# A hybrid RWKV-7 and sparse-attention layer: raised norms and masks, values behind transposes, and three reordered sums

## The chip, the core and the metric

The kernel runs on one core of one Trainium2 chip. The metric is the device time of one launch in microseconds (us), from the first to the last thing the core does. The engines have their own instruction queues: TensorE (PE) multiplies matrices into PSUM, VectorE (DVE) and ScalarE (ACT) work element by element and move PSUM results to SBUF, GpSimd (POOL) does a few small steps and issues some of the DMAs, SyncE (SP) issues most of the DMAs.

## The reference

One decoder layer on x of 1024 tokens by 1024 channels, float32. A projection feeds two mixers side by side; their outputs are gated, merged and followed by a feed-forward network (FFN).

```python
u = rmsnorm(x, norm1_g); p_rwkv, p_att, p_idx, p_gate = split(u @ w_in)
# RWKV-7, 8 heads of 64, on token-shifted p_rwkv: r, k, v, decay w, a, gate g
kk = (k * k_k) / max(norm(k * k_k, per head), 1e-12)
k = k * (1 + (a - 1) * k_a);  decay = exp(-exp(w))
# per token: sa = state @ -kk;  y = state @ r  after
state = state * decay + sa x (kk * a) + v x k
y_a = (groupnorm(y) + sum(r * k * r_k) * v) * g
# attention, 8 heads of 64: rope(q), rope(k), v; each query keeps the 256 keys
# with the highest indexer scores, softmax over them
y_b = dsa_attention(q, k, v, q_idx, k_idx, w_idx)
h = x + (sigmoid(g_a) * (y_a @ w_o_rwkv) + sigmoid(g_b) * (y_b @ w_o_att)) @ w_out
z_gate, z_up = split(rmsnorm(h, norm2_g) @ w_ffn_in)
h = h + (silu(z_gate) * z_up) @ w_ffn_out
return rmsnorm(h, normf_g)
```

## The kernel before

**Arithmetic.** Channels lie on the 128 partitions, tokens on the free axis, in two halves of 512 tokens. Each large matrix product is made of three products of values that are split into a high and a low part (`split`, L114 on ScalarE for the high part and L115 on VectorE for the low one): high × high (L140), high × low activation (L141), low weight × high (L145), in `mm3`. `mm3_last` (L149 to L158) puts the products that need the last block of the activations behind all others, for one or two outputs at a time. Weights come by DMA into `wst` and are split on the way.

**Order.** The order of TensorE's queue is that of the program (`manual_schedule`). The instructions of the other engines are put in order by a list scheduler when the kernel is built: among instructions that are ready by its own estimate it takes those within `tc.high_priority()` first, and otherwise the order of the program counts; on the chip each engine then runs its queue strictly in the order built. `weights` is in high priority already. `tc.issue_after(x)` keeps an instruction behind x in the built order.

**Filler.** RWKV is a chain of small dependent steps. `rwkv` runs it in four quarters of 256 tokens (q = 0 to 3; q = 0 and 1 are half 0), and between two steps it calls `pump(n)`, which takes work worth about n matmuls from the deque `fill`: projections in quarter 0, then projections of the gates (`proj_gates`), attention of half 0 blended with more gates (`blend`, 2 steps of one and 2 of the other), and from the middle of quarter 2 on (`ready`) the merge and the FFN of half 0. Attention of half 1 and the second merge and FFN come after RWKV. `ticks` pumps and also advances the late part of the indexer's selection (L944 among its lines) on VectorE and ScalarE.

**The steps of a quarter** that matter here: the sums of squares of the key per head (`sums`); the clamp into `nq` (L589, VectorE); two transposes of nq (L593, TensorE); the copy of 16 columns into `nr` (L595, VectorE); the power (L599, GpSimd); its split; two transposes (L604); the copy into `nrT` (L606, ScalarE); the spread back over channels (L612, TensorE) and the multiply into kk. Then come the operands AR (L630, L631) and BK (L637, L640) on VectorE, multiplies with the decays P and their inverse Pi. `km` is the key times its factor, multiplied ahead of the sums. Behind a pump follow eight masks in four pairs: TensorE makes products of BK and AR (L667) in two PSUM buffers, VectorE multiplies them with `cmask` into MT (L671); four groups of transposes of BK (L686) are copied into NAT by ScalarE (L689).

**PSUM.** `acc()` has three buffers, for large products; `mix()` has five, for everything else. A matmul into a buffer waits until its last reader is done.

**Attention** (`attend`) goes over 16 units of a half, (head pair, block of 128 queries). In one pass of the loop it makes the logits of unit i for two heads (L1029, reduced with the bias on VectorE in L1031, the exponential in L1034), transposes those of unit i-1 (`turn`, L1043, copied in L1045) and multiplies those of unit i-2 with v (`values`, L1053), with a `yield` behind each, at which the filler runs. The last results go through memory to `d_yb` (L1068 to L1090).

**The ends.** `merge` loads y (the RWKV half in blocks 0 to 3, the attention half in 4 to 7), splits it and multiplies it with `w_o`, the two halves into two accumulators (L1158 reads the first). `ffn_out` adds the FFN's output to h; the last of the three groups (`final`) also sums the squares of h (`Rms.add`) for the last norm. In half 1 this is `finish_out`, in two runs of 256 tokens. `Rms.columns` sums the squares over the partitions by a matmul with ones (L241) and takes the power on GpSimd.

## Time and profile before

| | |
|---|---|
| time, median of 3 runs | 1748.55 us (1747.58 to 1753.21) |
| the profiled execution's own time | 1748.71 us |
| its span | 1746.9 us |
| granted TensorE clock, mean | 0.996 |
| TensorE busy, matmuls | 1708.1 us, 98% |
| TensorE weight loads | 1410.3 us, 81% |
| VectorE busy | 1114.3 us, 64% |
| ScalarE busy | 833.3 us, 48% |
| GpSimd busy | 100.5 us, 6% |
| moved by DMA | 247.14 MB, 141 GB/s |

The page of the profile gives busy times and the chain of work that ended last. The list of waits has one row for each pair of a waiting instruction and what released it: the sum of the waits in us, how many, and the longest. The timeline has the start and the duration of each instruction, and in brackets how long its engine had been idle before it and what released it. The windows give the busy time of each engine in a stretch and the clock that TensorE was granted. The groups (by line and shape) give the total and the mean in ns.

### The profile page before, as it was taken

The numbers are of one execution on the slowest core, as the hardware profiler recorded it, in microseconds if no ns is written. First come the engines' busy times: TensorE is split into PE (matmuls) and PEld (weight loads), VectorE is DVE, ScalarE is ACT, GpSimd is POOL, SyncE is SP. The second block draws the span as 40 slices with busy tenths as digits, with TensorE's granted clock in tenths as the row PEclk, the third lists the DMA queues.
The fourth block names the chain that finished last, engine by engine and source line by source line (L and its number), as shares of the span: only waits on it lengthen the run. The fifth ranks groups of instructions, "written<-read, shape, count | busy, mean of one in ns | idle before, by whom it ended". The sixth has DMA issues, their size and how long they took to land.

```text
span 1746.9 us, 26692 instructions
## 1 busy us (share of the span) xinstructions
PE 1708.1 (98%) x10156; PEld 1410.3 (81%) x10156; DVE 1114.3 (64%) x2133; ACT 833.3 (48%) x1547; POOL 100.5 (6%) x123
## 2 busy tenths in 40 slices
PE   8999999999999998999999999999999999999997
PEld 6888888778878776878787888888788888888887
DVE  6789899857468567857876655445465564454464
ACT  6365998453445687645333455433234322232241
POOL 0000000010021111000100321000000000000000
PEclk9999999999999999999999999999999999999999
DMA  5542224536357535644343765173464344434442
GB/s 210 173 138 94 97 97 145 163 97 171 100 178 201 149 121 157 197 146 118 97 127 93 234 165 138 61 225 113 165 213 140 109 136 151 136 96 150 139 124 93
DMA packets 132383, 247.14 MB, mean 141 GB/s; under 512 B 36848, under 2 KB 60080, under 8 KB 132128
## 3 DMA queue, kind: packets, MB, share of 16 engines
q1 hardware_dynamic: 108896, 171.61, 31.7%
q10 hardware_dynamic: 15552, 47.75, 8.7%
q0 software_dynamic: 7808, 26.09, 5.6%
q8 instruction: 80, 1.31, 0.3%
q14 instruction: 47, 0.39, 0.1%
HBM read 192.40 MB, written 53.00 MB: 140 GB/s over the span
## 4 chain that ended last, share of the span: by engine, by line
PE 50%; issue 1%; DVE 1%; ACT 0%; POOLq 0%; POOL 0%; DVEq 0%; ACTq 0%
PE acc L145 14%; PE acc L140 13%; PE acc L141 13%; PE acc L156 3%; PE mix L1053 1%; PE mix L1029 1%; PE mix L1043 1%; PE acc L1197 0%; PE mix L800 0%; PE mix L788 0%; PE acc L1201 0%; ACT whi L114 0%; DVE h L1272 0%; PE mix L254 0%; PE mix L810 0%
## 5 line engine op out<-in xcount | busy, mean ns | idle before, releaser
L115 DVE TENSOR_TENSOR wlo<-wst,whi 128x1024 fp32r<-128x1024 f32 (+1 forms) x229 | 277.5, 1214 | 276.0 <-PE acc L145 132.7
L114 ACT ACTIVATE whi<-wst 128x1024 fp32r<-128x1024 f32 (+1 forms) x229 | 238.3, 1043 | 262.7 <-PE acc L141 186.9
L140 PE MATMUL acc<-zhi,whi 128*128 128x512 f32 x672 | 264.8, 394 | 0.0
L141 PE MATMUL acc<-zlo,whi 128*128 128x512 f32 x672 | 262.0, 390 | 0.0
L145 PE MATMUL acc<-zhi,wlo 128*128 128x512 f32 x672 | 170.2, 392 | 0.0
L140 PEld LDWEIGHTS acc<-zhi,whi 128*128 128x128 f32 x672 | 126.2, 188 | 26.8 <-issue 1.9
L141 PEld LDWEIGHTS acc<-zlo,whi 128*128 128x128 f32 x672 | 126.3, 188 | 24.8
L145 PEld LDWEIGHTS acc<-zhi,wlo 128*128 128x128 f32 x672 | 124.8, 188 | 25.4 <-issue 0.7
L140 PE MATMUL acc<-u1hi,whi 128*128 128x512 f32 x352 | 140.5, 399 | 0.1
L141 PE MATMUL acc<-u1lo,whi 128*128 128x512 f32 x352 | 137.6, 391 | 0.0
L140 PE MATMUL acc<-u0hi,whi 128*128 128x512 f32 (+1 forms) x352 | 135.5, 387 | 1.7 <-DVE tmp L323 1.7
L141 PE MATMUL acc<-u0lo,whi 128*128 128x512 f32 (+1 forms) x352 | 133.8, 383 | 0.0
L140 PE MATMUL acc<-fhi,whi 128*128 128x512 f32 (+1 forms) x318 | 114.3, 368 | 2.3 <-ACT whi L114 1.5
L141 PE MATMUL acc<-flo,whi 128*128 128x512 f32 (+1 forms) x318 | 112.9, 364 | 0.2 <-DVE flo L115 0.2
L145 PE MATMUL acc<-u1hi,wlo 128*128 128x512 f32 x352 | 90.0, 394 | 0.0
L145 PE MATMUL acc<-u0hi,wlo 128*128 128x512 f32 (+1 forms) x352 | 85.7, 384 | 0.0
L114 ACT ACTIVATE fhi<-tmp 128x512 fp32r<-128x512 f32 x44 | 27.7, 630 | 112.6 <-DVE tmp L1229 112.3
L140 PEld LDWEIGHTS acc<-u0hi,whi 128*128 128x128 f32 x352 | 66.2, 188 | 14.9 <-ACT stg L114 2.1
L140 PEld LDWEIGHTS acc<-u1hi,whi 128*128 128x128 f32 x352 | 66.2, 188 | 14.8 <-issue 1.3
L141 PEld LDWEIGHTS acc<-u1lo,whi 128*128 128x128 f32 x352 | 66.2, 188 | 12.6
L141 PEld LDWEIGHTS acc<-u0lo,whi 128*128 128x128 f32 x352 | 66.2, 188 | 12.1
L145 PEld LDWEIGHTS acc<-u1hi,wlo 128*128 128x128 f32 x352 | 64.9, 188 | 13.7 <-issue 0.9
(328 smaller groups left out, 3204.2 us busy)
## 6 DMA issues: line engine op xcount, KB each, us to landing
wst<-in_w_ffn_in SPq DMA_DIRECT2D x72, 512.0 KB, 3.6
wst<-in_w_in ACTq DMA_DIRECT2D x36, 512.0 KB, 4.5
wst<-in_w_in SPq DMA_DIRECT2D x27, 512.0 KB, 4.0
wst<-in_w_fo SPq DMA_DIRECT2D x25, 512.0 KB, 3.8
k<-d_k POOLq DMA_DIRECT2D x24, 512.0 KB, 7.9
h<-in_xT SPq DMA_DIRECT2D x32, 256.0 KB, 5.2
d_g<-tmp ACTq DMA_DIRECT2D x32, 256.0 KB, 3.4
tmp<-d_g SPq DMA_DIRECT2D x32, 256.0 KB, 3.7
```

Of the source, the lines that this page charges most:

```text
L114: A.activation(hi, x, AF.Copy)
L115: V.tensor_tensor(lo, x, hi.bitcast(F32), op=ALU.subtract)
L140: T.matmul(ps, whi[:, wk + k, :], ahi[:, ak + k, tok], start=k == 0, stop=False)
L141: T.matmul(ps, whi[:, wk + k, :], alo[:, ak + k, tok], start=False, stop=False)
L145: T.matmul(ps, wlo[:, wk + k, :], ahi[:, ak + k, tok], start=False, stop=k == nk - 1)
L156: T.matmul(ps, w[:, k, :], a[:, k, tok], start=k == 0 and w is whi and a is ahi, stop=k == nk - 1 and a is alo)
L1029: T.matmul(ps[:, :w], q[bi // 2][:, e, bi % 2 * 128:bi % 2 * 128 + 128], k[:, i, e, c:c + w], start=i == 0, stop=i == 1)
L1043: T.transpose(ps[:, j * 128:(j + 1) * 128], L[:, (c + j) * 128:(c + j + 1) * 128], ident)
L1053: T.matmul(py[64 * e:64 * e + 64, bi * 128:(bi + 1) * 128], v[:, j, 64 * e:64 * e + 64], pts[e][j // 4][:, j % 4, :], start=j == b, stop=j ...
```

## The change

1. `first_()` is a new name for high priority. It is put around the clamp, the copy into nr, the split of nr, the copy into nrT and the masks. `km*k` is issued behind the clamp.
2. The multiplies of r with the decays (half of AR), of km with their inverse (half of BK) and the scaling of ta stand ahead of the split of nr, which is issued behind the last of them.
3. The pumps around the norm are larger in places: 14 becomes 18, 18, 14, 14; 24, 26, 22, 26 become 28, 26, 22, 34; 10 becomes 10, 10, 10, 14 (quarters 0 to 3).
4. In `attend` the yield between the second transposes and the values goes, and the filler that it asked for is asked for behind the values. `blend` takes 4 steps of attention and 5 of gates.
5. In the first output block of half 0's merge `mm3_hi` makes all products with the high part of y first, for both accumulators, then those with the low part.
6. The final `ffn_out` uses `mm3_last` for its first output.
7. In the second run of `finish_out` the last block's squares are not added to the sum on VectorE; TensorE sums both tiles, in PSUM, and two scalings replace one.

```diff
+    def first_():
+        return tc.high_priority()
+    def mm3_hi(pss, w, act):
+        for a, ws in ((act[0], w), (act[1], w[:1])):
+            for i, ps in enumerate(pss):
+                for k in range(4 * i, 4 * i + 4):
+                    for x in ws:
+                        T.matmul(ps, x[:, k, :], a[:, k, :], start=a is act[0] and x is w[0] and k == 4 * i,
+                                 stop=a is act[1] and k == 4 * i + 3)
+                    yield len(ws)
...
-        def add(self, k):
+            self.parts = [self.acc]
+        def add(self, k, last=False):
...
+            elif last:
+                self.parts.append(tmp())
+                A.activation(self.parts[1][:, :n], self.h[:, k, self.tok], AF.Square)
...
-            ss, n = mix(), self.n
-            for t in range(n):
-                T.matmul(ss[:, 2 * t:2 * t + 2], self.acc[:, t * 128:(t + 1) * 128], ones[:, 0:2],
-                         start=True, stop=True)
+            n, ps = self.n, self.parts
+            sss = [mix() for _ in range(n if len(ps) > 1 else 1)]
+            for x in ps:
+                for t in range(n):
+                    T.matmul(sss[t % len(sss)][:, 2 * t:2 * t + 2], x[:, t * 128:(t + 1) * 128], ones[:, 0:2],
+                             start=x is ps[0], stop=x is ps[-1])
...
-            V.tensor_scalar(rs[:, :n], ss[:, 0:2 * n:2], 1.0 / D, 1e-6, op0=ALU.mult, op1=ALU.add)
+            m = len(sss)
+            for t, ss in enumerate(sss):
+                V.tensor_scalar(rs[:, t:n:m], ss[:, 2 * t:2 * n:2 * m], 1.0 / D, 1e-6, op0=ALU.mult, op1=ALU.add)
...
-            V.tensor_tensor(km, km, k, op=ALU.mult)
...
-            V.tensor_scalar(nq.rearrange("p a b -> p (a b)"), ps, 1e-24, None, op0=ALU.max)
-            pump(14)
+            with first_():
+                clamp = V.tensor_scalar(nq.rearrange("p a b -> p (a b)"), ps, 1e-24, None, op0=ALU.max)
+            with tc.issue_after(clamp.ins):
+                V.tensor_tensor(km, km, k, op=ALU.mult)
+            pump((18, 18, 14, 14)[q])
...
-            V.tensor_copy(nr.rearrange("p (t c e) -> p t c e", t=2, c=4),
-                          ps[:, 0:256].rearrange("p (t c k) -> p t c k", t=2, c=4)[:, :, :, 0:2])
+            with first_():
+                V.tensor_copy(nr.rearrange("p (t c e) -> p t c e", t=2, c=4),
+                              ps[:, 0:256].rearrange("p (t c k) -> p t c k", t=2, c=4)[:, :, :, 0:2])
...
-            split(nr2[:, :, 0, :].bitcast(F32R), nr2[:, :, 1, :].bitcast(F32R), nr3)
-            pump((24, 26, 22, 26)[q])
+            r4 = r.rearrange("p c (n t) -> p c n t", n=4)
+            for e in range(2):
+                V.tensor_tensor(AR[:, :, e::2, e, :], r4[:, :, e::2], P[:, :, e::2, 1:65], op=ALU.mult)
+            V.tensor_scalar(ta, ta, 0.5, 0.5, op0=ALU.mult, op1=ALU.add)
+            BK = [p.tile([128, 2, 2, 4, 64], F32, tag=f"BK{c}", name="BK") for c in range(2)]
+            for c in range(2):
+                s2 = slice(2 * c, 2 * c + 2)
+                before = V.tensor_tensor(BK[c][:, :, :, 0:4:3, :].rearrange("p c r s t -> p (c r) s t"),
+                                         km[:, s2, :].rearrange("p c (r s t) -> p (c r) s t", r=2, s=2),
+                                         Pi[:, s2, :].rearrange("p c (r s t) -> p (c r) s t", r=2, s=2), op=ALU.mult)
+            with first_(), tc.issue_after(before.ins):
+                split(nr2[:, :, 0, :].bitcast(F32R), nr2[:, :, 1, :].bitcast(F32R), nr3)
+            pump((28, 26, 22, 34)[q])
...
-            A.activation(nrT, ps[0:16, 0:256], AF.Copy)
-            pump(10)
+            with first_():
+                A.activation(nrT, ps[0:16, 0:256], AF.Copy)
+            pump((10, 10, 10, 14)[q])
...
                 for g in range(2):
-                    V.tensor_tensor(m[:, g::2, :], pss[g].rearrange("p (h t) -> p h t", h=4),
+                    with first_():
+                        V.tensor_tensor(m[:, g::2, :], pss[g].rearrange("p (h t) -> p h t", h=4),
...
                     ptss.setdefault(i - 1, []).append(turn(units[i - 1][1], Ls[i - 1][e]))
-                    yield 4 if half else (units[i - 1][1] + 3) // 2
+                    if e == 0 or i < 2:
+                        yield 4 if half else (units[i - 1][1] + 3) // 2
...
-                yield 4 if half else bi2 + 1
+                yield 8 if half else bi2 + 1 + (bi2 + 4) // 2
...
+            if d == 0 and half == 0:
+                pa, pb = acc(), acc()
+                yield from mm3_hi([pa, pb], w, yt)
+                V.scalar_tensor_tensor(ga, ga, 1.0, pa, op0=ALU.add, op1=ALU.mult)
+            else:
...
-        pss = []
-        if not final:
-            pss = [acc(), acc()]
-            yield from mm3_last(pss, [w(d) for d in range(2)], f, gn)
+        pss = [acc() for _ in range(1 if final else 2)]
+        yield from mm3_last(pss, [w(d) for d in range(len(pss))], f, gn)
...
-                    sq.add(d)
+                    sq.add(d, last=d == 7 and o > 0)
...
-        yield from blend(attend(0, at0[0][1], bias), gates, 2, 2)
+        yield from blend(attend(0, at0[0][1], bias), gates, 4, 5)
```

More of the change, by code (lines that the diff above doesn't have):

```diff
@@ L627, in rwkv @@
             kk4 = kk.rearrange("p c (n t) -> p c n t", n=4)
-            r4 = r.rearrange("p c (n t) -> p c n t", n=4)
             for e in range(2):
                 V.tensor_tensor(AR[:, :, e::2, 1 - e, :], kk4[:, :, e::2], P[:, :, e::2, 0:64], op=ALU.mult)
-                V.tensor_tensor(AR[:, :, e::2, e, :], r4[:, :, e::2], P[:, :, e::2, 1:65], op=ALU.mult)
-            V.tensor_scalar(ta, ta, 0.5, 0.5, op0=ALU.mult, op1=ALU.add)
             V.tensor_tensor(ta, ta, kk, op=ALU.mult)
-            BK = [p.tile([128, 2, 2, 4, 64], F32, tag=f"BK{c}", name="BK") for c in range(2)]
             for c in range(2):
@@ L639, in rwkv @@
                                 Pi[:, s2, :].rearrange("p c (r t) -> p (c r) t", r=2), op=ALU.mult)
-                V.tensor_tensor(BK[c][:, :, :, 0:4:3, :].rearrange("p c r s t -> p (c r) s t"),
-                                km[:, s2, :].rearrange("p c (r s t) -> p (c r) s t", r=2, s=2),
-                                Pi[:, s2, :].rearrange("p c (r s t) -> p (c r) s t", r=2, s=2), op=ALU.mult)
             rk = t4("x6")
@@ L670, in rwkv @@
                 for g in range(2):
-                    V.tensor_tensor(m[:, g::2, :], pss[g].rearrange("p (h t) -> p h t", h=4),
-                                    cmask[:, 64 - 64 * pa:192 - 64 * pa].unsqueeze(1).to_broadcast([128, 4, 128]),
-                                    op=ALU.mult)
+                    with first_():
+                        V.tensor_tensor(m[:, g::2, :], pss[g].rearrange("p (h t) -> p h t", h=4),
+                                        cmask[:, 64 - 64 * pa:192 - 64 * pa].unsqueeze(1).to_broadcast([128, 4, 128]),
+                                        op=ALU.mult)
                 MT.append(m)
@@ L1155, in merge @@
             SY.dma_start(gb, d_g[half][8 + d])
-            pa = acc()
-            yield from mm3(pa, w, yt, nk=4)
-            V.scalar_tensor_tensor(ga, ga, 1.0, pa, op0=ALU.add, op1=ALU.mult)
-            pb = acc()
-            yield from mm3(pb, w, yt, nk=4, wk=4, ak=4)
+            if d == 0 and half == 0:
[3 more added lines that the diff above has]
+            else:
+                pa = acc()
+                yield from mm3(pa, w, yt, nk=4)
+                V.scalar_tensor_tensor(ga, ga, 1.0, pa, op0=ALU.add, op1=ALU.mult)
+                pb = acc()
+                yield from mm3(pb, w, yt, nk=4, wk=4, ak=4)
             V.scalar_tensor_tensor(gb, gb, 1.0, pb, op0=ALU.add, op1=ALU.mult)
```

## The prediction

> **What bounds the kernel now.** The page comes first: the busy time of each engine, then the chain of work that ended last. Then who waited for whom on TensorE.

> ```profile
> PE 1708.1 (98%) x10156; PEld 1410.3 (81%) x10156; DVE 1114.3 (64%) x2133; ACT 833.3 (48%) x1547; POOL 100.5 (6%) x123
> PE 50%; issue 1%; DVE 1%; ACT 0%; POOLq 0%; POOL 0%; DVEq 0%; ACTq 0%
> ...
> PE mix L593 <- DVE nq L589: 2.6, 2, 1.5
> PE mix L612 <- ACT nrT L606: 2.4, 2, 1.7
> PE mix L686 <- ACT NAT L689: 2.2, 1, 2.2
> PE mix L604 <- DVE nr L115: 1.9, 2, 1.4
> PE mix L667 <- DVE MT L671: 1.6, 3, 0.8
> PE acc L140 <- DVE tmp L1158: 1.3, 2, 0.7
> PE mix L686 <- DVE MT L671: 1.3, 1, 1.3
> ```

> TensorE is busy for 98% of the span and carries the chain; the next step of the chain has 1%. The change takes away no large matmul, so only TensorE's idle time, 1746.9 - 1708.1 = 38.8 us, can shrink. Seven rows of the list of waits lie in the places that the change touches: the norm of RWKV's key (L593, L604, L612: 2.6, 1.9 and 2.4 us), its masks and the transposes behind them (L667, L686: 1.6, 1.3 and 2.2), and the first matmuls of the merge (L1158: 1.3), 13.3 us together. The second number of a row says how often, the third the longest.

> The timeline shows what makes such a wait. This is the norm in the third quarter, 512 to 767; each step is released by the one above it, and projections or attention should cover the gap.

> ```profile
> 659.46 0.17 DVE L595 COPY nr<-mix 128x16 f32<-128x16 f32 x1 [0.22 <-PE mix L593]
> 659.78 3.21 POOL L599 TENSOR_TENSOR nr<-nr,mhalf 128x16 f32<-128x16 f32 x1 [25.29 <-ACT z L953]
> 663.03 0.22 ACT L114 ACTIVATE nr<-nr 128x16 fp32r<-128x16 f32 x1 [2.61 <-POOL nr L599]
> 664.02 0.38 PE L604 MATMUL mix<-kc,nr 128*16 128x128 f32 x2
> 667.49 0.36 ACT L606 ACTIVATE nrT<-mix 16x256 fp32r<-16x256 f32 x1
> 667.90 0.73 PE L612 MATMUL mix<-nrT,ind 16*128 16x256 f32 x4 [1.66 <-ACT nrT L606]
> ```

> L604 is ready at 664.4, yet ScalarE copies its result only at 667.49: other work stood in its queue. The clock makes it dearer, by the windows around this wait and around the waits for NAT (behind the window stand its length, then the busy time of TensorE, its weight loads, VectorE, ScalarE and GpSimd, then the granted clock, 1.00 or 0.50):

> ```profile
> 665.50:668.90 3.40, 1.74 (x11) 1.14 (x10) 2.54 (x9) 3.40 (x8) 0.00 (x0) 1.00 0.88 323
> 668.90:672.30 3.40, 3.40 (x27) 3.07 (x27) 3.33 (x6) 2.94 (x8) 0.00 (x0) 0.50 0.48 164
> 682.60:686.00 3.40, 0.66 (x4) 0.42 (x4) 2.26 (x4) 2.26 (x5) 0.00 (x0) 1.00 0.88 234
> 686.00:689.40 3.40, 3.24 (x12) 2.66 (x13) 3.22 (x6) 3.16 (x8) 0.00 (x0) 0.50 0.31 61
> ```

> A stretch with only 1.74 us of matmuls in 3.40 is followed by 3.40 us at half clock, and so is one with 0.66. The second such stretch had 3.24 us of matmuls, so it lost about 3.24/2 = 1.6 us.

> A matmul of 512 columns in a stream costs 1.81/8 = 0.227 us:

> ```profile
> 873.32 1.81 PE acc L145 x8
> ```

> **The norms.** `first_` raises the clamp (L589), the small copy (L595) and the copy of nrT (L606); the multiplies of r, k and the inverse decays, which need no norm, move ahead of the split of nr; and more filler is pumped around the steps. In the built order on VectorE the clamp stands ahead of `km*k` in every quarter, where in the first and second it had stood behind it; two multiplies for BK and four for rk had stood ahead of it too in the first. With 16 matmuls instead of 12 behind the sums (16 × 0.227 = 3.6 us) the clamp is in time in the first three quarters; in the fourth there are 12 instead of 16, which I price at 0.3. So L593: -2.6 + 0.3 = **-2.3**. The power has 20 and 36 matmuls of projections ahead of L604 in the first and fourth quarter, besides transposes in the first, against 12 and 24 (in the first with transposes too): 8 × 0.227 = 1.8 us more, over the 0.5 and 1.4 that were waited there. But in the third quarter the copy at 659.46 now stands behind `km*k`, one AR multiply and a weight split; these take about 1.2, 0.7 and 1.2 us, of which attention's matmuls cover all but some 0.4. L604: -1.9 + 0.4 = **-1.5**.

> L612 is where the change does not do what it says. ScalarE runs its queue in the order built. In the third quarter eleven computing instructions now stand between the split of nr and the copy of nrT that was raised, three of them passes of the late selection (L944); eight, with one such pass, stood there before. Their durations:

> ```profile
> L944 ACT ACTIVATE junkl<-kept,z 128x1024 int8<-128x1024 f32 x16 | 18.2, 1138 | 0.0
> L944 ACT ACTIVATE junkl<-kept,z 128x896 int8<-128x896 f32 x16 | 16.5, 1032 | 0.1
> L1034 ACT ACTIVATE L<-L,mx 128x512 f32<-128x512 f32 x8 | 5.8, 719 | 3.1 <-DVE mx L1031 3.0
> L1045 ACT ACTIVATE pt<-mix 128x512 f32<-128x512 f32 x48 | 27.1, 586 | 17.7 <-PE mix L1043 17.7
> L486 ACT ACTIVATE tmp<-tmp 128x512 f32<-128x512 f32 x32 | 20.2, 630 | 40.7 <-DVE tmp L485 40.7
> ```

> 1.1 + 2 × 1.0 + 0.7 + 3 × 0.5 + 0.6 + 5 small ones near 0.2 come to about 6.7 us from the split to the copy, against 667.49 - 663.03 = 4.5. TensorE has 2 us of work behind L604 and none besides, so L612 waits about 4.9 us where it waited 1.7; the first stretch at half clock stays. In the fourth quarter a gate's copy no longer stands ahead of nrT and the 0.8 goes. L612: -2.4 + 4.9 = **+2.5**. The bounds are 0 (selection done early, while ScalarE waits for the power) and 6.

> **The masks.** In the third quarter TensorE waited 0.6 us for a mask ahead of L667, then ahead of L686 1.3 for a mask and 2.2 for NAT, 4.1 together; the other 1.0 of L667 fell in the fourth.

> ```profile
> 674.92 1.09 PE L1068 MATMUL mix<-kc,ri 128*64 128x128 f32 x16
> 677.54 0.32 SPq L1090 DMA_DIRECT2D d_yb<-tmp  x1
> 683.14 1.25 ACT L114 ACTIVATE yhi<-ylo 128x512 fp32r<-128x512 f32 x2 [2.11 <-DMA ylo<-d_yb]
> 686.16 2.12 PE L686 MATMUL mix<-kc,BK 128*128 128x128 f32 x8 [2.24 <-ACT NAT L689]
> 687.93 0.78 PE L140 MATMUL acc<-yhi,whi 128*128 128x512 f32 x1
> ```

> The last step of attention (L1068) goes through memory (L1090) into y, and its splits stood on VectorE ahead of three masks, on ScalarE ahead of NAT. Masks hold the PSUM buffers that the transposes (L686) need. In the new order three splits stand among the masks, those of the RWKV half of y, which came from memory long before; the five others follow all masks. NAT's copies stand behind all eight splits of ScalarE, but then the four transposes find free buffers among five, since every mask is done. What comes late next is the merge, and `mm3_hi` lets it start with eight matmuls on the RWKV half and eight on the high attention half, 3.6 us, before it needs a low part. The masks remain a chain of their own:

> ```profile
> L671 DVE TENSOR_TENSOR MT<-mix,cmask 128x512 f32<-128x512 f32 x32 | 19.9, 681 | 6.9 <-PE mix L667 6.9
> L115 DVE TENSOR_TENSOR wlo<-wst,whi 128x1024 fp32r<-128x1024 f32 x213 | 262.3, 1233 | 264.5 <-PE acc L145 125.7 <-ACT whi L114 103.3 <-ACT UV L802 7.0
> ```

> Eight masks and three splits at 0.6 us apiece (0.68 with what overlaps) are 7 us against 6.3 us of matmuls and transposes, so some 1.0 us stays. -4.1 + 1.0, and -1.5 for the second stretch at half clock (its 1.6, less a little for matmuls that then run in the gap): **-4.6**. In the fourth quarter a weight split and three multiplies of the FFN, 1.2 + 3 × 0.6, are built ahead of or between the masks, since eight more matmuls of it have run: its 1.0 us of waits for masks grow, and the second quarter's transposes of v meet three logits in the same buffers: **+1.0**.

> **The merge and the two FFN ends.** L1158 frees the bank of the second d's last product. It now has 36 matmuls (8.2 us) instead of about as many with the masks running late into them; five small steps that wait for the DMA of N stand ahead of it on VectorE. I keep 0.5: **-0.8**. For the last FFN group of half 0, `mm3_last` puts 15 matmuls (3.4 us) ahead of the last f instead of 10:

> ```profile
> 1250.61 0.50 PE L140 MATMUL acc<-fhi,whi 128*128 128x512 f32 x1 [0.83 <-ACT fhi L114]
> ```

> The 0.83 and 0.2 behind it go, as 5 × 0.227 covers them: **-1.0**. After such a wait the first matmul also takes 0.50 where one in a stream takes 0.40; 14 waits fewer or shorter by that are **-1.4**.

> **The tail.** This add goes off the path, since TensorE sums both parts; a second scaling of one column (0.1) comes onto it. **-0.4**; nothing else runs there.

> ```profile
> 1737.10 0.43 DVE L235 TENSOR_TENSOR sacc<-sacc,tmp 128x256 f32<-128x256 f32 x1 [0.54 <-ACT tmp L234]
> ```

> **Attention.** Values behind transposes save at most one change of kind of matmul for each unit:

> ```profile
> 1051.66 0.40 PE L141 MATMUL acc<-zlo,whi 128*128 128x512 f32 x1
> 1051.99 1.31 PE L1053 MATMUL mix<-pt,v 128*64 128x128 f32 x20
> ```

> The values start 0.33 us after the last projection, not 0.23. But by the page's pair of groups the transposes need no such gap and the values need theirs on both sides, so I take 0, with bounds 0 and 32 × 0.1 = 3.2 us. The filler moved behind is the same work. `blend` with 4 and 5 puts four steps of attention in a row, then 20 projections; its operands are older by a whole burst, so I price a longer hold on PSUM buffers at **+0.5**.

> **Power beside multiplies.** The power on GpSimd took longer where VectorE worked:

> ```profile
> 365.42 2.92 POOL L599 TENSOR_TENSOR nr<-nr,mhalf 128x16 f32<-128x16 f32 x1 [110.74 <-DVE nr L595]
> 830.50 4.35 POOL L599 TENSOR_TENSOR nr<-nr,mhalf 128x16 f32<-128x16 f32 x1 [19.50 <-ACT tmp L1226]
> 660.78 1.21 DVE L115 TENSOR_TENSOR wlo<-wst,whi 128x1024 fp32r<-128x1024 f32 x1
> ```

> 2.92 in the second quarter with VectorE idle, 3.21 in the third and 4.35 in the fourth with it busy; the weight split is one of the third's neighbours. The change puts the AR and BK multiplies beside the power in every quarter, which may stretch it by up to 4.35 - 2.92 = 1.4 us. The added matmuls ahead of L604 (8 × 0.227 = 1.8 us in the first and fourth quarter) hide that; in the third nothing was added, and there I take a third of 1.4: **+0.5**. Bounds 0 and 3.3, if it shows in three quarters.

> **Sum.** -2.3 - 1.5 + 2.5 - 4.6 + 1.0 - 0.8 - 1.0 - 1.4 - 0.4 + 0.5 + 0.5 = -7.5. The profiled execution took 1748.71 us (1746.9 of span), 0.16 over the median of 1748.55; so 1741.2 against its own time, and **1741.0** against the median.

> [...]

> **Rivals.** *Nothing waits for nrT* (0.16): the selection passes run while ScalarE waits for the power, 659.78 to 663.03, and L612 waits for nothing. For it: ScalarE was idle for much of that time. Against: its queue is in order and they stand behind the split. -7.5 - 4.9 = -12.4: 1736.

> *The waits come back* (0.10): DMA of y is no earlier (from L1068 to the end of ScalarE's last split 9.5 us passed, 674.92 to 683.14 + 1.25, and none of that is shortened), and the merge waits for y instead of NAT. The 4.1 us of waits return at another line: -7.5 + 4.1 = -3.4, 1745.

> [...]

> *Slower: bursts of attention* (0.12). Four steps in a row ask for four to five PSUM buffers, which VectorE and ScalarE must have emptied. Once in the old order a logit matmul found none:

> ```profile
> 588.38 0.51 PE L1029 MATMUL mix<-k,q 128*128 128x256 f32 x2 [0.84 <-DVE mx L1031]
> ```

> At 0.84 us in each of the 16 units of half 0 that is 13.4 us: 1741.0 + 13.4 = 1754.4. It decides from 7.5/16 = 0.47 us a unit. Against: 20 projections (4.5 us) between bursts empty the buffers.

> **How the numbers follow.** The forecast has 0.57, its own range 1736 to 1746 by the bounds of L612 (-2.5, +1.1), of the power (+2.8) and of the attention's values (up to -3.2). 0.3% (5.2 us, about what a measurement of this kernel can tell from no change) puts faster below 1743.3 and slower above 1753.8. Some 0.46 of the forecast's 0.57 lies below 1743.3, with the first rival's 0.16 that is 0.62; the rest of the forecast, 0.11, and the second and third rival, 0.15, are 0.26 within; the bursts are 0.12. The range for 8 in 10 leaves out the bursts and the far ends of the first rival and the third: 1732 to 1750.

> **What would show it.** In the list of waits: L593 under 0.5, L604 under 0.8, L612 near 5 with ScalarE's nrT behind L944 in the third quarter, NAT and its 2.2 gone, one stretch at half clock there instead of two, no wait at the start of the last FFN group. I am wrong if L612 waits under 2, if waits for y on ScalarE stand at the start of the merge, or if logits wait in many units.

## The result: slower by 0.3%

The changed kernel took 1758.41 us in the median of six runs (1754.72 to 1760.33), the kernel before 1750.82 (six runs, 1747.58 to 1754.01). The ratio on record is 1.0032, with a 95% interval of 1.0018 to 1.0046; the quotient of the two medians is 1.0043, inside that interval. The forecast was 1741.0, with a range of 1732 to 1750.

These lines of the page of the profile after answer to those quoted of before:

```profile
span 1756.1 us, 26688 instructions
PE 1715.3 (98%) x10160; PEld 1418.7 (81%) x10160; DVE 1111.9 (63%) x2133; ACT 832.9 (47%) x1547; POOL 106.4 (6%) x123
PE 77%; DVE 10%; ACT 6%; issue 3%; DMA 2%; POOL 1%; SPq 0%; ACTq 0%; DVEq 0%; POOLq 0%
```

The span grew by 9.2 us (1746.9 to 1756.1). TensorE's idle time is 1756.1 - 1715.3 = 40.8 us against 38.8, only 2.0 more. The rest, 7.2 us, is TensorE's *busy* time, 1715.3 against 1708.1, for practically the same number of matmuls (10160 and 10156 in the page). Matmuls got slower: the granted clock, followed along the trace, was at one half for 20.5 us between the start and the tail, in stretches of 3.41 and 6.83 us, where before it was so for 6.8 (two stretches of 3.41). In the first of these stretches a projection's matmul starts 0.43 us behind the one ahead of it (671.37 to 671.80), at full clock 0.23 us (675.07 to 675.30); so about half the time at half clock is lost, (20.5 - 6.8)/2 = 6.9 us by this estimate. Some 1.8 us of the 9.2 lie in the first 350 us, ahead of the first step that the change touches, where full clock came 5.5 us later (15.6 against 10.1 us): that is the start of an execution and not the change (TensorE's waits for the first operand u0hi, 7.1 us before and 7.5 after, were 7.0 to 7.7 us in the runs below, 7.3 where nothing but the ends was changed).

The list of waits on TensorE, after:

```profile
...
PE mix L1077 <- ACT L L1068: 4.4, 2, 4.3
PE acc L144 <- DVE tmp L1194: 3.0, 1, 3.0
...
PE mix L652 <- ACT nrT L646: 2.0, 2, 1.2
PE mix L700 <- DVE MT L705: 1.8, 3, 0.6
PE mix L643 <- DVE nr L115: 1.8, 2, 1.2
...
PE mix L700 <- ACT bs L683: 1.7, 2, 1.1
PE mix L790 <- ACT TZ L772: 1.7, 3, 0.8
...
PE mix L261 <- ACT tmp L249: 0.7, 1, 0.7
```

Lines have moved: L593, L604 and L612 of before are L617, L643 and L652; L667 and L686 are L700 and L720; L1158 is L1194; L1034 and L1043 of attention are L1068 and L1077; L756 is L790. The waits for nq (2.6), NAT (2.2) and the last f (0.8) of before are gone. Two have grown most: transposes of attention wait 4.4 us for their exponential, 4.3 of it at once, where the sum was 0.4 before, and the merge waits 3.0 us for the first read of an accumulator, where the longest was 0.7. The windows around the two show what they cost:

```profile
664.16:667.57 3.41, 0.00 (x0) 0.00 (x0) 3.09 (x9) 1.29 (x4) 2.05 (x1) 1.00 0.39 148
667.57:670.98 3.41, 2.72 (x17) 2.06 (x18) 1.38 (x6) 3.41 (x11) 0.00 (x0) 0.50 0.20 77
698.29:701.70 3.41, 1.07 (x5) 0.56 (x3) 2.14 (x7) 3.13 (x10) 0.86 (x1) 1.00 0.83 294
701.70:705.12 3.42, 2.79 (x7) 2.22 (x8) 3.35 (x10) 3.42 (x9) 0.00 (x0) 0.50 0.57 178
```

TensorE stood still for one whole window (0.00 busy) and worked for 1.07 us of the other, and behind each of them the clock was at 0.50. Each low stretch lasted two windows, to 674.4 and to 708.5. Two more windows at half clock, from 766.6 and 865.5, lie behind the end of half 0's attention (680.2), among short waits for TZ and for masks.

The timeline shows where the first of the two comes from:

```profile
663.31 2.90 POOL L624 TENSOR_TENSOR nr<-nr,mhalf 128x16 f32<-128x16 f32 x1 [22.91 <-DVE nr L620]
664.28 1.29 DVE L635 TENSOR_TENSOR BK<-x,x 128x512 f32<-128x512 f32 x2
665.49 0.68 DVE L1065 CUSTOM_DVE_ANT_0 L<-mix,bias 128x512 f32<-128x512 f32 x1
666.25 0.21 ACT L114 ACTIVATE nr<-nr 128x16 fp32r<-128x16 f32 x1 [2.63 <-POOL nr L624]
667.39 0.72 ACT L1068 ACTIVATE L<-L,mx 128x512 f32<-128x512 f32 x1
668.26 1.11 PE L1077 MATMUL mix<-kc,L 128*128 128x128 f32 x4 [4.26 <-ACT L L1068]
```

This is the norm of the third quarter. Right behind the transposes of nq came a whole burst of attention, logits, transposes, values, transposes, with no projection in it. VectorE reduced the last logits (L1065) only behind the AR and BK multiplies that the change had moved there; ScalarE had the split of nr ahead of the exponential in its queue and idled 2.63 us for the power. The exponential came at 667.39, and all the projections that could have covered the gap stood on TensorE behind the burst.

The second, at the merge's start, by the timeline:

```profile
699.42 1.23 DVE L115 TENSOR_TENSOR wlo<-wst,whi 128x1024 fp32r<-128x1024 f32 x1 [4.08 <-ACT whi L114]
701.60 0.68 DVE L1194 SCALAR_TENSOR_TENSOR tmp<-tmp,acc 128x512 f32<-128x512 f32 x1
702.33 0.80 PE L144 MATMUL acc<-yhi,whi 128*128 128x512 f32 x1 [2.96 <-DVE tmp L1194]
```

TensorE needs the accumulator that L1194 reads; that read stands on VectorE behind a weight split, which had itself waited 4.08 us for ScalarE, and behind steps on N.

### The profile page after: what moved, and what is told of

It is laid out like the page before. It is cut to its first block, busy times and chain, and to the rows that moved or that the text cites. A ratio compares the mean times of both kernels' runs of the same rounds, so it can differ in the third digit from the quotient of the medians.

```text
span 1756.1 us, 26688 instructions
## 1 busy us (share of the span) xinstructions
PE 1715.3 (98%) x10160; PEld 1418.7 (81%) x10160; DVE 1111.9 (63%) x2133; ACT 832.9 (47%) x1547; POOL 106.4 (6%) x123
## 3 DMA queue, kind: packets, MB, share of 16 engines
q8 instruction: 80, 1.31, 0.3%
## 4 chain that ended last, share of the span: by engine, by line
PE 77%; DVE 10%; ACT 6%; issue 3%; DMA 2%; POOL 1%; SPq 0%; ACTq 0%; DVEq 0%; POOLq 0%
PE acc L144 19%; PE acc L149 19%; PE acc L145 19%; PE acc L160 3%; PE mix L928 2%; PE mix L1087 2%; DVE wlo L115 2%; ACT junk L978 2%; PE mix L1063 2%; PE mix L1077 2%; ACT junkl L978 1%; DVE junk L975 1%; PE mix L834 1%; PE mix L822 1%; PE acc L1237 1%
## 5 line engine op out<-in xcount | busy, mean ns | idle before, releaser
L115 DVE TENSOR_TENSOR wlo<-wst,whi 128x1024 fp32r<-128x1024 f32 (+1 forms) x229 | 275.5, 1206 | 284.7 <-PE acc L149 124.0
L114 ACT ACTIVATE whi<-wst 128x1024 fp32r<-128x1024 f32 (+1 forms) x229 | 238.1, 1043 | 241.1 <-PE acc L145 176.1
L145 PE MATMUL acc<-zlo,whi 128*128 128x512 f32 x672 | 261.9, 390 | 0.0
L145 PEld LDWEIGHTS acc<-zlo,whi 128*128 128x128 f32 x672 | 126.2, 188 | 25.3
L145 PE MATMUL acc<-u1lo,whi 128*128 128x512 f32 x352 | 138.3, 393 | 0.0
L145 PE MATMUL acc<-u0lo,whi 128*128 128x512 f32 (+1 forms) x352 | 133.7, 382 | 0.0
L145 PE MATMUL acc<-flo,whi 128*128 128x512 f32 (+1 forms) x312 | 110.5, 363 | 0.0
L114 ACT ACTIVATE fhi<-tmp 128x512 fp32r<-128x512 f32 x44 | 27.8, 632 | 118.2 <-DVE tmp L1269 118.2
L145 PEld LDWEIGHTS acc<-u1lo,whi 128*128 128x128 f32 x352 | 66.7, 190 | 12.9
L145 PEld LDWEIGHTS acc<-u0lo,whi 128*128 128x128 f32 x352 | 66.2, 188 | 12.2
```

The costliest lines, as they stand in the source:

```text
L114: A.activation(hi, x, AF.Copy)
L115: V.tensor_tensor(lo, x, hi.bitcast(F32), op=ALU.subtract)
L145: T.matmul(ps, whi[:, wk + k, :], alo[:, ak + k, tok], start=False, stop=False)
```

## The experiments

The theory from these traces was that the new attention, by its bursts, leaves TensorE without cover where RWKV or the merge is late, and that the clock then adds about as much again (at the merge 3.0 us of wait and, by estimate, 6.8/2 = 3.4 us for the 6.83 us at half clock behind it). The rivals were the raised norm steps, and `mm3_hi` for the merge. Line numbers are those of the changed kernel unless said otherwise; all ratios are to the kernel before, with their 95% intervals.

### Four parts undone

The merge's first block in the old order:

```diff
-            if d == 0 and half == 0:
+            if False:
```

> The changed kernel, but the first block of the merge uses the old order of products. The theory that mm3_hi is half of the loss (its first accumulator is read by a VectorE step that is queued behind five steps waiting for N, so the third accumulator is late: 3.0 us, then two windows of 3.4 us at half clock) expects the wait of 3.0 and the slow windows behind it gone and the old waits of 1.3 us back: 3.0 + 3.4 - 1.3 = about 5 us less than the changed kernel, so about even with the kernel before (ratio 1.000). The rival, that the attention order alone makes the loss, expects the merge to be late anyway (y comes late): no more than 1 us less, ratio 1.003.

Measured: 1.0052 (1.0033 to 1.0071). The waits for the exponential (4.4) and at the merge (2.9, 2.5 of it at once) are both there, so `mm3_hi` is not what made the second. The theory that it was half of the loss fell.

The old norm steps, from the multiply of km to the last of BK, with the old pumps:

> The changed kernel with the old norm steps (order, priorities and pumps), masks and the rest as changed. If the raised split of nr and the multiplies ahead of it made the 4.3 us wait of the transposes for the exponential in the third quarter, that wait and its slow windows go (4.3 + 3.4) and the norm's old waits come back (6.9 of before against 3.8, and 1.7 of half clock): about 3 us less than the changed kernel, ratio 1.0015. If the attention order made it, the exponential still stands behind the split of nr on ScalarE (in the built order one of the last two does) and the waits of the norm come on top: 1 to 3 us more, ratio 1.004 to 1.005.

Measured: 1.0090 (1.0071 to 1.0110), worse than either expectation. With the bursts in place the raised norm steps help by about 0.6%: taking them away brought waits of 5.2 us (L1102, the last product of an attention unit, released by L1065, the reader of logits) and 4.6 us (L1194) and 30.7 us at half clock (granted clock 0.989 in the mean).

The old attention:

```diff
-                    if e == 0 or i < 2:
+                    if True:
...
-                yield 8 if half else bi2 + 1 + (bi2 + 4) // 2
+                yield 4 if half else bi2 + 1
...
-        yield from blend(attend(0, at0[0][1], bias), gates, 4, 5)
+        yield from blend(attend(0, at0[0][1], bias), gates, 2, 2)
```

> The changed kernel with the old order of attention and the old blend of 2 and 2. If attention's order made the 4.3 us wait for the exponential, it goes with its slow windows (7.7), since in the built order both last exponentials stand ahead of the split of nr: ratio about 0.999. If the norm steps made it, a wait of the same kind stays on another line (nrT or the exponential): ratio 1.003.

Measured: 0.9979 (0.9967 to 0.9991), 1746.66 us: faster than both kernels. TensorE's busy time is back at 1708.1 us, with 3.4 us at half clock (granted clock 0.997 in the mean, 0.992 after), and the list of waits has lost both of the new leaders:

```profile
span 1743.9 us, 26695 instructions
PE 1708.1 (98%) x10160; PEld 1410.4 (81%) x10160; DVE 1116.2 (64%) x2133; ACT 832.6 (48%) x1547; POOL 106.4 (6%) x123
...
PE mix L700 <- ACT tmp L508: 2.7, 1, 2.7
PE mix L1077 <- ACT L L1068: 2.6, 1, 2.6
```

A wait of 2.6 us for an exponential is left, but it is another one, in the second quarter. So the attention is the cause of the loss; the next runs had to say which half of it. The rest of the change then wins 0.21%, 3.7 us, where the sum without the attention's +0.5 had forecast 8.0.

The two ends alone, on the kernel before:

> The kernel before with only the two ends changed: the first output of the last FFN group in mm3_last, and the last square summed on TensorE. By the prediction -1.0 for the group and -0.4 for the square, so 1.4 us less than before, ratio 0.9992; the waits at the start of that group (0.8 and 0.2) gone and the wait of the last sum 1.6 us shorter by 0.4. A rival expects the second accumulation and the second scaling to take back the 0.4: -1.0, ratio 0.9994.

Measured: 0.9993 (0.9980 to 1.0005). The time can't tell this from no change; in the trace the waits for the last f are gone and that of the last sum is 0.7 instead of 1.6.

### Which half of the attention, and what the rest is worth

Values directly behind transposes kept, blend 2 and 2:

```diff
-        yield from blend(attend(0, at0[0][1], bias), gates, 4, 5)
+        yield from blend(attend(0, at0[0][1], bias), gates, 2, 2)
```

> The changed kernel with the old blend of 2 and 2, but values still directly behind the transposes. If the loss comes from the bursts of four attention steps (in the third quarter a whole burst lies between the transposes of nq and nr, with no projection in it, and its last exponential stands on ScalarE behind the split that waits for the power), it goes here, since in the built order attention is over before that norm: the waits of 4.3 and 3.0 us and three of the four slow stretches go, ratio 0.997 to 0.999. If the loss comes from taking away the projections between transposes and values, it stays: ratio 1.003, with waits of the values (L1087) for the copies of the transposes in many units.

Measured: 0.9990 (0.9980 to 0.9999). The wait for the exponential is gone, the one at the merge is still there, and the transposes of nr (L643) wait up to 2.6 us:

```profile
PE acc L144 <- DVE tmp L1194: 4.7, 1, 4.7
PE mix L643 <- DVE nr L115: 4.3, 3, 2.6
```

The reverse, old yields and blend 4 and 5:

> The changed kernel with the old yields (projections between transposes and values) and the new blend of 4 and 5. If bursts make the loss it stays or grows, since a unit is again five steps and attention falls behind the gates: ratio 1.003 to 1.006. If the order of values made it: about 0.998.

Measured: 1.0047 (1.0030 to 1.0064). Now one of the values' matmuls waits for a copy of transposes, and the clock is at half for 20.5 us again (0.993 in the mean).

```profile
PE mix L1087 <- ACT pt L1079: 5.2, 1, 5.2
```

The blend alone, on the kernel before:

```diff
-        yield from blend(attend(0, at0[0][1], bias), gates, 2, 2)
+        yield from blend(attend(0, at0[0][1], bias), gates, 4, 5)
```

> The kernel before with the blend of 4 and 5 as the only change. If bursts of attention lose by themselves (a burst with no projection in it beside a norm or a mask leaves TensorE to wait, and the clock is halved behind it), this is slower by 5 us or more: ratio 1.003 to 1.006, with a wait of 2 us or more in an attention step. If they lose only because the raised norm steps stand ahead of the attention's exponential, it is even: 1.000.

Measured: 1.0069 (1.0054 to 1.0084), 1761.76 us. This one edit costs more than the whole change. Its waits are not long, but spread over RWKV's steps and attention (line numbers of the kernel before; the traced execution, 1765.2 us, was the slowest of the five):

```profile
span 1763.4 us, 26678 instructions
PE 1721.7 (98%) x10156; PEld 1421.7 (81%) x10156; DVE 1116.6 (63%) x2133; ACT 833.6 (47%) x1547; POOL 100.3 (6%) x123
...
PE mix L593 <- DVE nq L589: 3.6, 2, 2.4
PE mix L667 <- DVE MT L671: 2.7, 3, 1.6
PE mix L1043 <- ACT L L1034: 2.2, 1, 2.2
PE mix L756 <- ACT TZ L738: 2.1, 4, 1.5
```

The four rows grew by 1.0, 1.1, 1.8 and 1.7 us, while that of L612 fell by 1.6. Busy time is up by 13.6 us (1721.7 against 1708.1) and idle time by 2.9, with 34.1 us at half clock (0.988 in the mean). One of the places, by the windows and the timeline:

```profile
596.13:599.54 3.41, 1.72 (x38) 1.09 (x36) 0.39 (x1) 2.42 (x5) 0.00 (x0) 1.00 0.50 183
599.54:602.95 3.41, 3.30 (x53) 3.03 (x48) 0.15 (x1) 3.31 (x8) 0.00 (x0) 0.50 0.00 0
598.54 0.24 PE L756 MATMUL mix<-TT,TZ 32*32 32x32 f32 x2 [1.53 <-ACT TZ L738]
```

A wait of 1.53 us left 1.72 us of matmuls in its window, and three windows at half clock followed, to 609.8.

The size of a burst was not all that these three runs changed. With the old yields a unit of attention takes five steps, without the yield four. So the kernel before, the changed kernel and the run with the old attention all take one unit to five steps of the gates; the run with the old blend takes one to four, and the two runs with old yields and 4 and 5 one to 6.25. Attention of half 0 ends at 673.0 us before, 680.2 after and 672.4 with the old attention, but at 654.4, 684.4 and 687.0 in those three. How much of their differences comes from bursts and how much from attention that runs earlier or later, no run separates; the pair of the changed kernel and the old attention, with the same pace, is free of this.

Old attention and old norm, with the new masks, merge and ends:

> Old attention (order and blend) and the old norm steps, with the new masks, merge and ends: beside the run with old attention alone it tells what the norm steps are worth. By the prediction L593 and L604 give 3.8 less, L612 took 2.5 and the power 0.5, so the norm is worth 0.8 and this kernel is 0.8 above that run, ratio 0.9984. By the waits that the two traces of the first runs show (7.1 us of norm waits in the run with the ends alone, 2.9 in the one with old attention, where a wait of 2.7 for BK is new) it is worth 1.5; with a stretch at half clock 3.2, ratio 0.9998.

Measured: 0.9991 (0.9981 to 1.0001). Beside 0.9979 the norm is worth about 0.12%, 2 us; the two intervals overlap.

Old attention, masks without priority:

```diff
-                    with first_():
+                    with nullcontext():
...
```

> Old attention and masks without their priority, with the new norm, merge and ends: what the masks are worth. By the prediction 3.6 us (the waits for masks and NAT, 4.1 us in the third quarter less 1.0, 1.5 of half clock, less 1.0 in the fourth): ratio 1.000, with waits of L720 for NAT and MT of 2 us or more back. If the waits were NAT's because attention's result came late, and not the masks' order, they come back less: ratio 0.9985.

Measured: 1.0011 (1.0001 to 1.0021). Beside 0.9979 the priority of the masks is worth 0.32%, 5.6 us; most of it again is clock, 13.7 us at half against 3.4 (0.994 in the mean against 0.997).

The masks' own wait came back (L700 for MT, 3.3 us in three, 2.1 at once; 1.8 and 0.6 with priority), but no wait for NAT and none of L720, against the expectation. In this one trace two of the three extra low windows, from 682.1 and 859.6, follow waits that the run with the old attention has as well (2.7 us; 0.6, 0.5 and 0.6 us), there with full clock behind them; only the one from 688.9 follows the new wait of 2.1. How much of the 5.6 us belongs to the masks and how much to where the windows fell is not shown.

### The wait at the merge

Five of the traces had a wait of 2.5 us or more there by then, the others at most 0.8. The first try gave the merge's first block two other PSUM buffers, the second also freed the split of nr:

```diff
-                pa, pb = acc(), acc()
+                pa, pb = mix(), mix()
...
-            with first_(), tc.issue_after(before.ins):
+            with first_():
...
```

> The changed kernel with the old blend of 2 and 2, and with the first block of the merge accumulating in two of the five small-purpose PSUM buffers instead of two of the three large ones. If the merge's wait (4.7 us for L1194 in the run with the old blend alone, and two slow windows behind it) comes from the third large buffer being held behind VectorE's queue, which waits for N, it shrinks to 1.5 or less and the slow windows go: 4.7 - 1.5 + 3.4 = 6.6 us less than that run, ratio 0.9955. If the merge is held by the weights or by y instead, the wait appears at another line of it: ratio 0.998 to 0.999.

> As the run with the merge in the small buffers, and the split of nr no longer kept behind the last BK multiply. If L643's wait of 2.6 us in the third quarter comes from that order (VectorE's low split stands behind BK, BK behind the exponential Pi, and Pi behind the high split on ScalarE, which waits for the power), it goes, with the slow window behind it: 4.3 us less, ratio 0.993. If VectorE, which now waits for the power ahead of AR and BK, makes the masks late instead, L700 waits 2 us or more and nothing is won: 0.9955.

Measured: 1.0010 (0.9997 to 1.0023) and 0.9997 (0.9986 to 1.0008), both missed. The merge's wait did shrink, from 4.7 to 1.8 and 2.1 us, and L643's longest from 2.6 to 0.6 in the second; but waits for TZ (L769, 1.9 and 1.8 us), NAT (1.7 and 1.2) and, in the second, BK (L700, 1.7) and nrT (L652, 3.3 in two) came, and 10.2 us at half clock near 760. On VectorE a second weight split, which idles 2.8 us for ScalarE, and reads of the merge now stand ahead of most of RWKV's steps on N; the first of these starts at 701.1 and 701.5 us, where the run with the old blend had it at 696.6. The second's trace is of its slowest execution (1754.03 us, the median is 1748.98), so its waits count for less than its ratio.

The next aimed at the 2.7 us wait of L700 in the run with the old attention:

```diff
-            pump((10, 10, 10, 14)[q])
+            pump((10, 10, 2, 14)[q])
...
```

> The run with the old attention, with the third quarter's pump between nrT and its spread cut from 10 to 2, so that eight projections (8 x 0.227 = 1.8 us) run behind the spread and the transposes of v instead of ahead of them. That run's wait of 2.7 us ahead of the first masked products (L700), for BK on VectorE, should fall by the 1.8 that VectorE's chain starts earlier: 0.9 left, ratio 0.997. If nrT or the weight split (which waits for ScalarE) that now stands ahead of BK is late instead, the wait moves there: ratio 0.998.

Measured: 1.0022 (1.0013 to 1.0030). At the masks it did about what was expected: they came 2.0 us earlier against the transposes of nr, and their wait fell from 2.7 to 1.1. But the edit also changed the order that the scheduler built on VectorE 10 us later. The timeline of the run with the old attention, and then of this one:

```profile
693.75 0.69 DVE L1194 SCALAR_TENSOR_TENSOR tmp<-tmp,acc 128x512 f32<-128x512 f32 x1 [1.05 <-PE acc L170]
696.85 1.23 DVE L115 TENSOR_TENSOR wlo<-wst,whi 128x1024 fp32r<-128x1024 f32 x1
699.20 0.18 DVE L739 TENSOR_TENSOR tw<-W,N 128x31 f32<-128x31 f32 x1
```

```profile
698.72 1.36 DVE L115 TENSOR_TENSOR wlo<-wst,whi 128x1024 fp32r<-128x1024 f32 x1 [5.81 <-ACT whi L114]
700.00 0.18 DVE L739 TENSOR_TENSOR tw<-W,N 128x31 f32<-128x31 f32 x1
701.03 0.68 DVE L1194 SCALAR_TENSOR_TENSOR tmp<-tmp,acc 128x512 f32<-128x512 f32 x1
701.76 0.79 PE L144 MATMUL acc<-yhi,whi 128*128 128x512 f32 x1 [5.52 <-DVE tmp L1194]
```

In the first the read (L1194) stands ahead of a weight split and the steps on N and runs when its accumulator is done. In the second it stands behind both, VectorE sits idle 5.81 us for the high part of the weights on ScalarE, and TensorE waits 5.52 us for the accumulator. The built orders of all runs that use the old buffers divide the same way: with the split and three products of N ahead of the read (the changed kernel and five runs: the old merge, the old norm, the old blend, old attention with old norm, and this one) the longest wait there was 2.5 to 5.5 us, with the split alone ahead (the kernel before, the ends alone, the blend alone) 0.7 to 0.8, and with the read first (the old attention, with and without masks, and the old yields) there was none.

Two more runs were made on this. Weight split pinned behind the read:

```diff
-                w = weights(ins["w_o"][d])
+                with tc.issue_after(first_read.ins) if half == 0 and d == 2 else nullcontext():
+                    w = weights(ins["w_o"][d])
...
```

> The run with the later filler, with the weight split of the merge's third block built behind the read of the first accumulator on VectorE (L1195 here). If the wait of 5.5 us at the merge comes from the queue order (the split stands ahead of that read and waits 5.8 us for the high part on ScalarE), the read now stands only behind five small steps that wait for N: the wait falls to about 2, with one slow window less: 3.5 + 1.7 = 5.2 us, ratio 0.999. If N's arrival sets it and not the split, the wait stays at 4 to 5 us, ratio 1.002.

Measured: 1.0006 (0.9996 to 1.0015).

```profile
699.09 0.20 DVE L739 TENSOR_TENSOR tw<-W,N 128x31 f32<-128x31 f32 x1 [5.33 <-DMA N<-d_n]
700.14 0.68 DVE L1195 SCALAR_TENSOR_TENSOR tmp<-tmp,acc 128x512 f32<-128x512 f32 x1
700.87 0.50 PE L144 MATMUL acc<-yhi,whi 128*128 128x512 f32 x1 [3.77 <-DVE tmp L1195]
```

The wait fell from 5.5 to 3.8 and one slow window went, less than expected: the steps on N, still ahead of the read, wait for their DMA until 699.09. So the queue's order makes the wait, by the weight split and by N, and in these two traces N has the larger part.

> The run with the old attention, with the old order of products in the merge's first block. In both built orders the first read of the merge stands ahead of the weight split and of the steps that wait for N. If mm3_hi is worth what the prediction gave it, the merge's low parts of y come late here: 0.8 us more and no new wait over 1 us, ratio 0.9984 to 0.999. If mm3_hi costs, since it holds the first accumulator for 28 matmuls instead of 12, this is faster: 0.997.

Measured: 0.9985 (0.9974 to 0.9996), within the error of the run with the new merge (0.9979), and no wait at the merge. `mm3_hi` itself is worth at most a microsecond or two, which these runs don't resolve.

The fastest version is the changed kernel with the old attention, 0.21% below the kernel before.

## Why the prediction was wrong

**The attention** is the step that failed. It was priced at +0.5, "a longer hold on PSUM buffers". Between the changed kernel and the one with the old attention lie 1.0032 and 0.9979, 0.53% or 9.3 us, and the blend alone cost 12 us (0.69%). The rival *Slower: bursts of attention* had the right edit and sign, with a chance of 0.12, but in the main the wrong mechanism: it looked for missing buffers in each of 16 units. The changed kernel's list has four waits, 2.1 us in all, that L1065, the reader of logits, released (0.8 before); only beside the old norm did one take 5.2. What the runs showed in its place is a wait of 4.3 us of attention itself, at the norm of the third quarter, and low windows behind it and behind the merge: of the 12.2 us between the traces of these two kernels 5.0 are idle time and 7.2 slower matmuls. The reading that fits is that bursts cost where *RWKV* waits: with 2 and 2 a short pump brought some projections, which need nothing but weights; with 4 and 5 it brings either a burst, whose steps themselves wait for VectorE and ScalarE, or a long row of projections. The wait of 4.3 us shows this in one place; the two low windows behind the end of attention it does not explain.

**The clock.** The prediction counted two stretches at half clock in one place, and priced all other waits by their length. It should have asked of every new wait how little it leaves of matmuls in a window. In each of the traces of before and after the low stretches lie on a grid of 3.413 us: before the second starts 5 steps behind the first (668.90 and 685.97), after they start 10, 29 and 58 steps behind the first (667.57; 701.70, 766.56 and 865.54). Of the windows of this grid at full clock, in these two traces and in two places of the one of the blend alone, all 4 with less than 1.5 us of matmuls were followed by half clock (0.00, 0.66 and 1.07, and 1.20 from 524.45 with the blend alone), and so were all 3 with 1.5 to 2.0 us (1.69, 1.72 and 1.76). Of 10 with 2.0 to 2.5 us in the first two traces none was, of 24 with 2.5 to 3.0 us one (2.52), so the busy time of a window alone does not draw the edge. (Ends of matmuls are modelled in a trace, so these edges are soft.) A wait of about 2 us thus costs, by an estimate from half of 3.41 us, some 1.7 us more for each low window behind it, one to three of them in these places, or nothing, by where it falls. The 1.53 us wait above was followed by three.

**L612** was to wait 4.9 us in the third quarter behind the selection. L652, its new line, waited there not at all; its 2.0 us are 0.8 in the second quarter and 1.2 in the fourth. TensorE reached it late, since it stood at the exponential, and the selection passes were done by then. The forecast counted what stands in ScalarE's queue, not what TensorE would be held by meanwhile. With the old attention it waited not at all there either: in that built order the copy of nrT came 2.6 us after the split (669.50 to 672.09), with no pass between. So the rival *Nothing waits for nrT* was right about this wait, for other reasons than its own. The figure of 4.9 doesn't follow from its rows either: 6.7 instead of 4.5 us from the split to the copy makes 1.7 + 2.2 = 3.9. And in the fourth quarter 0.8 was to go, and 1.2 came.

**L593** fell as forecast (2.6 to nothing). **L604** was to keep 0.4, in the third quarter, and L643, its new line, kept 1.8: 0.6 in the second and 1.2 in the fourth, each released by the split behind a longer power.

```profile
515.56 5.04 POOL L624 TENSOR_TENSOR nr<-nr,mhalf 128x16 f32<-128x16 f32 x1 [6.35 <-DVE nr L620]
838.91 6.76 POOL L624 TENSOR_TENSOR nr<-nr,mhalf 128x16 f32<-128x16 f32 x1 [18.52 <-DVE nr L620]
```

Before, the four powers took 2.92, 3.23, 3.21 and 4.35 us (the first, at 365.42, is the first quarter's and not the second's, as the prediction has it); after, 3.03, 5.04, 2.90 and 6.76. So **the power** grew by up to 2.4 us, more than the 1.4 that the added matmuls were to hide, and not in the third quarter, where it was priced. The second quarter's took 3.23 before and 5.04 after. The multiplies beside it kept their length (two of BK in 1.29 us at 841.62, inside the power of 6.76; 1.28 before at 517.25, with no power beside them), so no run shows VectorE held by the power, which the third rival had a share of the chances for; what stands in its place is a longer power. Why the power grows in the second and fourth quarter beside the same multiplies that leave the third's at 2.90 stays open. The whole norm, forecast at -0.8 with the power, is worth about 2 us with the old attention, within the two intervals.

**The masks** were forecast at -4.6 + 1.0 = -3.6 and gave 5.6 us with the old attention and the new norm. NAT's wait is gone and the chain of masks leaves 1.8 + 0.5; but NAT's wait is also gone in the run without the priority, so it is not this that removed it, and the gain lies in the masks' own wait and the clock. A wait of 1.7 for bs or BK ahead of them was not foreseen.

**The merge** was priced at 0.5 left; 3.0 and two slow windows came. The five small steps ahead of the read had been seen in the built order. They were set against 8.2 us of matmuls; the weight split ahead of them, which waits for ScalarE (4.08 us in the changed kernel), and the late arrival of N were left out. The rival *The waits come back* looked for them at y: no wait for y stands in the changed kernel's list.

**The ends**: -1.0 and -0.4 forecast; the waits give -1.0 and -0.9, the time -0.07% (not resolved).

**The parts** do not add up: beside the old norm steps (0.9991) the new masks and merge win nothing over the ends alone (0.9993), beside the new ones the masks' priority wins 5.6 us. With each trace the waits at the merge and the place of the low windows change too, and a sum of single waits has no term for that.

What stays open, besides: why the built order puts the read first in some variants and last in others; no run here shows it.

## What to carry to other kernels

Where an in-order engine is kept busy by filler beside a chain of dependent steps, mix the filler finely: work that depends on nothing must be on hand at each wait, and a burst of work that has waits of its own was no cover here (4.3 us of wait). Look at busy time as well as idle time after a change: here idle time grew by 2 us and the same matmuls took 7 us longer, with 20.5 us at half clock instead of 6.8. And in a kernel whose queues a scheduler orders, check after each edit where the reads that free a full pool have landed; a small edit 10 us away moved one behind a wait of 5 us.

## What the runs showed of the hardware that was not expected

The power on GpSimd of the same 128x16 values took from 2.90 to 6.76 us over the traces of before and after.
